# A down-projection by Strassen's seven products in a hybrid encoder layer on one core

## The chip, the cores and the metric

The kernel runs on one core of a Trainium2 chip. The metric is device time in microseconds, the median of several executions. TensorE (PE) multiplies into banks of PSUM; VectorE (DVE) and ScalarE (ACT) read the banks and work on SBUF; GpSimd (POOL) works on SBUF alone; SyncE (SP) issues most DMAs. Each engine carries out its own instructions in order and waits for the others by semaphores.

## The reference, cut to what matters

The layer has a token-mixing sublayer (mLSTM and Mamba-2 branches) and a gated MLP. The change touches the MLP:

```python
u = causal_dwconv(x @ w_up[l], f_conv_w[l], f_conv_b[l])      # width 3 over the tokens
u_gate, u_val = jnp.split(u, 2, -1)
x = layer_norm(ALPHA * x + (jax.nn.silu(u_gate) * u_val) @ w_down[l], ln2_g[l], ln2_b[l])
```

There are 512 tokens, 1024 model columns and D_FF = 2752 hidden features, that is 21.5 tiles of 128. `w_up` is 1024 x 5504 and `w_down` 2752 x 1024, all in float32.

## The kernel before

**Precision.** Each float32 operand is split in two: H, a copy rounded to the type that TensorE takes (a cast on ScalarE), and L, the remainder (a subtraction on VectorE). A product of two operands is three matmuls: H by H, L by H, H by L.

**Weights.** The host lays all weights out as units of 128x1024 in the order of use. `advance` (L132) loads unit after unit into three `raw` buffers (DMA issued by SP, L136), casts it to `wH` (L159) and subtracts to `wL` (L165); `wH` and `wL` have three buffers each. A unit's split waits until TensorE has finished with the unit three before it.

**Up-projection** (the loop over j = 0..20 that calls `feature_major` and `conv_taps`). A gate unit and a value unit of 128 columns each take 24 matmuls (8 tiles of the model dimension, three each) into one bank. Four banks (`mm_bank`) rotate. `conv_taps` (L503) reads a bank three times: ScalarE scales the bank into a `tmp` tile (L505), VectorE adds two shifted taps (L507). ScalarE's SiLU (L1050), VectorE's product (L1051) and a split (L1053, L1054) give the tiles `fH`, `fL` of 128 features by 512 tokens. A last unit `um` holds the half tile of both kinds. `tmp` tiles have eight buffers.

**Down-projection** (`wide_product`, L929, with `tail=5`). All eight banks hold the output: four token tiles c by two column halves hf. Feature tile after feature tile, each bank gets three matmuls of 128x512 (L944); the half tile, stacked as H over L, gets two. The last five feature tiles are done bank by bank, so that the layer norm of a token tile (`wd`, L1087, and the block below it) runs beside the matmuls of the next. The tiles `x1r` hold the residual, read back from DRAM at the end of the up-projection and scaled there (L1076 to L1078).

**Order.** The tile framework's scheduler orders each engine's instructions by a simulated timeline. Inside `in_order(...)` blocks the engines that are named keep the order in which the code is written; the last one covers PE, DVE, ACT and POOL from the last five feature tiles to the end. A pool's buffer is given out again once its last readers are done.

## Time and profile before

| | |
|---|---|
| median of 3 runs | 942.72 us (942.71 to 942.82) |
| profiled execution, its time | 942.7 us |
| its span | 941.0 us |
| TensorE busy | 924.0 us, 98% |
| VectorE, ScalarE, GpSimd busy | 555.0, 382.3, 66.0 us |
| granted TensorE clock, mean | 0.994 |
| DMA | 105.13 MB, 112 GB/s |

The span runs from the first to the last instruction. Rows of a timeline read: start, duration, engine, line, operation, output<-inputs, count, and in brackets the idle time before it and what ended that. Rows of a group end with busy time, mean ns of one, and idle time before. Rows of a stretch (A:B) give its length and for PE, weight load, DVE, ACT and POOL the busy time and count, then the granted clock, the mean busy share of the DMA engines and GB/s. Rows of DMA issues end with the microseconds from issue to landing. In a row of waits stand the total, the count and the longest.

### The profile page before, as it was taken

What the parts mean: (1) busy time and instruction counts of PE and PEld (TensorE: products, weight loads), DVE (VectorE), ACT (ScalarE), POOL (GpSimd) and SP (SyncE); (2) the same over time, 40 slices, a digit from 0 to 9 for tenths busy, and PEclk for the clock granted to TensorE, in tenths of its full rate; (3) what the DMA queues carried; (4) which work ended last, traced back from release to release, by engine and by line L of the source; (5) the groups of instructions that cost most, each with busy time, mean ns of one, the idle gap of its engine ahead of it and who ended that gap; (6) DMA issues with size and microseconds to landing.
All of it is one profiled execution on the core that took longest, in us unless ns stands there. A gap on an engine that the chain in (4) does not pass through costs nothing.

```text
span 941.0 us, 11703 instructions
## 1 busy us (share of the span) xinstructions
PE 924.0 (98%) x4565; PEld 762.3 (81%) x4565; DVE 555.0 (59%) x916; ACT 382.3 (41%) x572; POOL 66.0 (7%) x81
## 2 busy tenths in 40 slices
PE   7999999999999999999999999999999999999996
PEld 4988888888877888888888888888888888878884
DVE  6685889873556465324339467666666556642246
ACT  4456456442664552234122235544444444332121
POOL 3000000211012510000000000000000000000005
PEclk8999999999999999999999999999999999999998
DMA  5334326453232432223334352222322322632212
GB/s 186 105 101 138 109 88 142 123 147 118 90 111 70 139 109 77 102 90 96 106 112 157 112 178 91 90 90 92 109 90 93 110 90 91 251 128 90 95 62 90
DMA packets 46311, 105.13 MB, mean 112 GB/s; under 512 B 4064, under 2 KB 21144, under 8 KB 46256
## 3 DMA queue, kind: packets, MB, share of 16 engines
q1 hardware_dynamic: 45456, 103.30, 34.0%
q0 software_dynamic: 512, 1.07, 0.4%
q8 instruction: 36, 0.59, 0.3%
q14 instruction: 19, 0.16, 0.1%
q10 hardware_dynamic: 288, 0.02, 0.0%
HBM read 100.08 MB, written 4.30 MB: 111 GB/s over the span
## 4 chain that ended last, share of the span: by engine, by line
PE 94%; DVE 2%; DMA 1%; issue 1%; POOL 0%; ACT 0%; DVEq 0%; ACTq 0%; POOLq 0%
PE u L185 23%; PE wd L944 10%; PE g L185 9%; PE z L185 5%; PE o L185 5%; PE v L575 5%; PE xs L185 5%; PE pb L185 5%; PE pa L185 5%; PE wo L944 4%; PE bc L185 4%; PE q L185 2%; PE k L185 2%; PE bc L335 1%; PE up L185 1%
## 5 line engine op out<-in xcount | busy, mean ns | idle before, releaser
L165 DVE TENSOR_TENSOR wL<-raw,wH 128x1024 fp32r<-128x1024 f32 x151 | 186.4, 1238 | 231.3 <-ACT wH L159 229.2
L159 ACT CAST wH<-raw 128x1024 fp32r<-128x1024 f32 x152 | 159.1, 1051 | 285.5 <-PE g L185 62.8
L185 PE MATMUL u<-x1H,wL 128*128 128x512 f32 x312 | 121.4, 389 | 0.0
L185 PE MATMUL u<-x1L,wH 128*128 128x512 f32 x312 | 121.4, 389 | 0.0
L185 PE MATMUL u<-x1H,wH 128*128 128x512 f32 x312 | 121.4, 389 | 0.0
L185 PEld LDWEIGHTS u<-x1H,wH 128*128 128x128 f32 x312 | 58.6, 188 | 12.1
L185 PEld LDWEIGHTS u<-x1H,wL 128*128 128x128 f32 x312 | 58.6, 188 | 12.0
L185 PEld LDWEIGHTS u<-x1L,wH 128*128 128x128 f32 x312 | 58.6, 188 | 11.8
L944 PE MATMUL wd<-wH,fH 128*128 128x512 f32 x168 | 65.5, 390 | 0.8 <-ACT wH L159 0.8
L944 PE MATMUL wd<-wH,fL 128*128 128x512 f32 x168 | 65.4, 389 | 0.0
L944 PE MATMUL wd<-wL,fH 128*128 128x512 f32 x168 | 63.9, 389 | 0.0
L185 PE MATMUL g<-xnH,wH 128*128 128x512 f32 x128 | 50.1, 392 | 0.0
L185 PE MATMUL g<-xnH,wL 128*128 128x512 f32 x128 | 49.8, 389 | 0.0
L185 PE MATMUL g<-xnL,wH 128*128 128x512 f32 x128 | 49.8, 389 | 0.0
L232 POOL TENSOR_TENSOR rs<-ve,mhalf 128x1 f32<-128x1 f32 x12 | 7.6, 629 | 555.8 <-DVE ve L256 555.5
L944 PEld LDWEIGHTS wd<-wH,fH 128*128 128x128 f32 x168 | 31.5, 188 | 7.7 <-ACT wH L159 1.2
L944 PEld LDWEIGHTS wd<-wH,fL 128*128 128x128 f32 x168 | 31.5, 188 | 6.6
L944 PEld LDWEIGHTS wd<-wL,fH 128*128 128x128 f32 x168 | 31.5, 188 | 6.5
L1053 ACT CAST fH<-cg 128x512 fp32r<-128x512 f32 x21 | 13.0, 620 | 53.0 <-DVE cg L1051 53.0
L507 DVE SCALAR_TENSOR_TENSOR cv<-u,par,cv 128x511 f32<-128x511 f32 (+1 forms) x40 | 29.8, 746 | 0.7
L1050 ACT ACTIVATE cg<-cg 128x512 f32<-128x512 f32 x21 | 13.3, 632 | 40.8 <-DVE cg L507 40.8
L507 DVE SCALAR_TENSOR_TENSOR cg<-u,par,cg 128x511 f32<-128x511 f32 (+1 forms) x38 | 28.4, 746 | 0.6
(326 smaller groups left out, 1972.2 us busy)
## 6 DMA issues: line engine op xcount, KB each, us to landing
raw<-in_wts_dram SPq DMA_DIRECT2D x154, 512.0 KB, 3.3
csb<-scr SPq DMA_DIRECT2D x8, 512.0 KB, 7.3
gt<-in_prow_dram SPq DMA_DIRECT2D x12, 256.0 KB, 4.7
xt<-in_x_dram SPq DMA_DIRECT2D x4, 512.0 KB, 6.5
rb<-scr SPq DMA_DIRECT2D x4, 512.0 KB, 5.5
res<-in_x_dram SPq DMA_DIRECT2D x4, 512.0 KB, 5.3
x1d<-res SPq DMA_DIRECT2D x4, 512.0 KB, 2.6
x1r<-x1d SPq DMA_DIRECT2D x8, 256.0 KB, 5.7
```

The lines of the kernel that those rows point to most:

```text
L159: nc.scalar.copy(H, raw)
L165: eng.tensor_tensor(L, raw, H.bitcast(F32), ALU.subtract)
L185: nc.tensor.matmul(ps[:, t0:t1], w_[:, k, :], a_[k][:, t0:t1], start=i == 0, stop=i == 3 * KD - 1)
L232: nc.gpsimd.tensor_tensor(dst, var, epsl[:, :n], ALU.pow)
L335: nc.tensor.matmul(fb[u][:, t], w_[:, k, :], a_[k][:, t], start=n == 1, stop=n == 3 * KD)
L507: nc.vector.scalar_tensor_tensor(dst[:, d:], ps[:, 0:T - d], prm(ws[n - 1 - d], j)[rows], dst[:, d:], ALU.mult, ALU.add)
L575: nc.tensor.matmul(banks[c], a_[k][:, cs_], w_[:, kk, :], start=first and s == 0, stop=last and s == 2)
L944: nc.tensor.matmul(banks[c, hf], a_[:, cs_], w_, start=k == 0 and s == 0, stop=k == n - 1 and s == len(prs) - 1)
L1050: nc.scalar.activation(tg, tg, AF.Silu)
L1053: nc.scalar.copy(H, tg)
```

## The change

Twenty of the feature tiles are multiplied by Strassen's scheme in Winograd's form. With the tokens in halves (256 each), the features in halves (ten tiles each) and the output columns in halves (512 each), the activations are A11, A12, A21, A22 and the weights B11, B12, B21, B22. The sums are S1 = A21 - A22, S2 = S1 - A11, S3 = A11 - A21, S4 = S2 + A12, T1 = B11 + B12, T2 = T1 + B22, T3 = B22 + B12, T4 = T2 + B21; the products P1 = A11 B11, P2 = A12 B21, P3 = S4 B22, P4 = A22 T4, P5 = S1 T1, P6 = S2 T2, P7 = S3 T3. A product covers two token tiles (two banks) and has five steps of two feature tiles, 12 matmuls each. P6 and P7 are accumulated on the bank of P1, P3 on that of P5; after a product the banks are read and added to, or subtracted from, `x1r`. The remaining one and a half feature tiles ("r") are multiplied as before, four matmul groups on four bank pairs.

The four activation sums are made by GpSimd in the up-projection, whose order of units alternates between the feature halves (`UP_ORDER`). They are split (H and L) in the down-projection. The four weight sums are made by DMAs issued by GpSimd from DRAM to DRAM, copies and accumulating ones, in six stages for each of five blocks, two feature tiles to a block; GpSimd keeps the order of the code there. The residual is scaled and shifted in the up-projection and stored to DRAM (`residual`). The whole down-projection stands in an `in_order` block. P4's last three steps run first for token tile 2, then for token tile 3. For token tiles 0 and 1 the last bias is added by an accumulating DMA.

TensorE where the up-projection ends and the down-projection begins, before (`um` is the last up unit, `wd00` the bank of token tile 0 and column half 0, `x1H7` and `x1L7` the activations; the rows ahead are alike in both):

```order
L185 MATMUL um_6491<-x1L7_4420,wH131_6418 128x512
L185 MATMUL um_6491<-x1H7_4412,wL131_6419 128x512
L944 MATMUL wd00_6583<-wH132_6449,fH0_5004 128x512
L944 MATMUL wd00_6583<-wH132_6449,fL0_5005 128x512
L944 MATMUL wd00_6583<-wL132_6450,fH0_5004 128x512
L944 MATMUL wd01_6584<-wH132_6449,fH0_5004 128x512
L944 MATMUL wd01_6584<-wH132_6449,fL0_5005 128x512
```

and now, with what the rows wait for (`dnH20` is the split weight block of P2's step 0, `a2H0` activations of A12, `wdy0` and `wdy1` the two banks of P2):

```order
L178 MATMUL um_6575<-x1H7_4412,wL131_6509 128x512
L1219 MATMUL wdy0_6643<-dnH20_6665,a2L0_5066 128x512
L1219 MATMUL wdy0_6643<-dnL20_6666,a2H0_5065 128x512 [waits DVE_49]
L1219 MATMUL wdy1_6644<-dnH20_6665,a2H0_5065 128x512 [waits DVE_49,Activation_49]
L1219 MATMUL wdy1_6644<-dnH20_6665,a2L0_5066 128x512
```

The first bank pair is now the one that rotates in after `um`: `wdy1` is given `um`'s bank and waits for VectorE and ScalarE at the stage's fourth matmul.

ScalarE near the end, before (`wH152` and `wH153` are the last weight splits, `x1r00` the output tile of token tile 0 and column half 0):

```order
L159 CAST wH150_7073<-raw150_7011 128x1024
L159 CAST wH152_7111<-raw152_7071 128x1024
L159 CAST wH153_7115<-raw153_7101 128x1024
L1115 ACTIVATE x1r00_6541<-x1r00_6541,nb2_0_7160,rs2_6582 128x512
L1115 ACTIVATE x1r01_6545<-x1r01_6545,nb2_0_7160,rs2_6582 128x512
```

and now (`dnH42` to `dnH44` are the splits of P4's steps 2 to 4):

```order
L1053 CAST dnH41_7314<-dn41_7294 128x1024
L1053 CAST dnH42_7334<-dn42_7312 128x1024
L1249 ACTIVATE x1r00_6611<-x1r00_6611,nb2_0_7352,rs2_6636 128x512
L1249 ACTIVATE x1r01_6613<-x1r01_6613,nb2_0_7352,rs2_6636 128x512
L1053 CAST dnH43_7364<-dn43_7332 128x1024
L1053 CAST dnH44_7382<-dn44_7362 128x1024
L1249 ACTIVATE x1r10_6615<-x1r10_6615,nb2_1_7386,rs2_6636 128x512
```

The normalisations of token tile 0 moved ahead of the last two weight splits.

GpSimd in the up-projection had nothing to do before. A turn of it now, with waits (`sum2` holds S1 to S4, `tsum0` to `tsum3` are T1, T2, T3 and T4; a DMA at L1085 accumulates, one at L1087 copies):

```order
L1085 DMA tsum1_5015<-in_wts_dram 128x2x512 [waits DMASW6_49]
L1087 DMA tsum0_5014<-in_wts_dram 128x2x512
L1087 DMA tsum2_5016<-in_wts_dram 128x2x512
L1087 DMA tsum3_5017<-tsum1_5015 128x1024 [waits DMASW7_49]
L1085 DMA tsum0_5014<-in_wts_dram 128x2x512 [waits DMASW0_49]
L1085 DMA tsum2_5016<-in_wts_dram 128x2x512 [waits DMASW4_49,DMASW1_49]
L1103 TENSOR_TENSOR sum2_5006<-cg4_5624,cg14_5701 128x256 [waits DVE_49]
L1104 TENSOR_TENSOR sum2_5006<-sum2_5006,cg4_5624 128x256 [waits Pool_49]
L1105 TENSOR_TENSOR sum2_5006<-cg4_5624 128x256
L1106 TENSOR_TENSOR sum2_5006<-sum2_5006,cg14_5701 128x256 [waits Pool_49]
L1085 DMA tsum3_5017<-in_wts_dram 128x2x512 [waits DMASW5_49,DMASW2_49]
```

The additions that release the `tmp` tiles `cg` stand in one order with DMAs that wait for earlier DMAs (the semaphores DMASW).

The diff, cut to its core:

```diff
+UP_ORDER = [j for i in range(10) for j in (i, i + 10)] + [20]
...
+    def block(k0, hf, i):
+        return wts[DN[k0 + 2 * i]:DN[k0 + 2 * i] + 2, :, 512 * hf:512 * hf + 512].rearrange("u p c -> p u c")
+
+    def weight_sum(stage, i):
...
+        t1, t2, t3, t4 = (t[:, i] for t in tsum)
+        moves = [[(t1, block(0, 0, i), False), (t3, block(10, 1, i), False)],
+                 [(t1, block(0, 1, i), True), (t3, block(0, 1, i), True)],
+                 [(t2, t1, False)], [(t2, block(10, 1, i), True)], [(t4, t2, False)], [(t4, block(10, 0, i), True)]]
+        for dst, src, add in moves[stage]:
+            if add:
+                nc.gpsimd.dma_start(dst, src, accum_op=ALU.add)
+            else:
+                nc.gpsimd.dma_start(dst, src)
+
+    with in_order(ET.Pool):
+        for i, j in enumerate(UP_ORDER):
+            tg = gated(i, j)
+            if i in (3, 5, 7, 9):
+                residual((i - 3) // 2)
...
+                nc.gpsimd.tensor_tensor(s1, low[:, TH:], tg[:, TH:], ALU.subtract)
+                nc.gpsimd.tensor_tensor(s2, s1, low[:, 0:TH], ALU.subtract)
+                nc.gpsimd.tensor_tensor(s3, low[:, 0:TH], low[:, TH:], ALU.subtract)
+                nc.gpsimd.tensor_tensor(s4, s2, tg[:, 0:TH], ALU.add)
...
+            for stage in range(5, -1, -1):
+                if (i - 1 - stage) % 3 == 0:
+                    weight_sum(stage, (i - 1 - stage) // 3)
...
-    wd_tail = wide_product(UX["DN"], fH, fL, 5, "wd", last_stack=True)
+    bX, bY = ([mm_bank(f"wd{n}{i}") for i in range(2)] for n in "xy")
+    bZ, bW = ([sm_bank(f"wd{n}{i}") for i in range(2)] for n in "zw")
+    BANK = {1: bX, 2: bY, 3: bZ, 4: bW, 5: bZ, 6: bX, 7: bX}
+    steps = ([(2, 0), (2, 1), (2, 2), ("r", 0), ("r", 1), (2, 3), (2, 4)] + [(1, i) for i in range(5)]
+             + [(5, i) for i in range(5)]
+             + [(6, 0), (6, 1), (3, 0), (6, 2), (3, 1), (6, 3), (3, 2), (6, 4), (3, 3), (3, 4)]
+             + [(7, i) for i in range(5)] + [(4, i) for i in range(5)])
...
+    def ahead(n):
+        for what, f, m in (("load", load_step, n + 3), ("hl", split_step, n + 2), ("s", sum_step, n + 2)):
...
+        for q in range(2):
+            for m in ms:
+                for s_, (a_, w_) in enumerate(((aH, H), (aL, H), (aH, L))):
+                    nc.tensor.matmul(BANK[p][m], a_[:, q, m * P:(m + 1) * P], w_[:, q, :],
...
+            elif (p, i) == (7, 4):
+                scaled(bX, 2, 0)
+            elif (p, i) == (4, 0):
+                plus(bX, 2, 1, op=ALU.subtract)
+                apply2(0)
+            elif (p, i) == (4, 1):
+                for c in (2, 3):
+                    nc.vector.bn_stats(bn2[c][:, 1, :], x1r[c][1])
+                ahead(len(steps) - 1)
+                apply2(1)
...
+        def last(c):
+            for p, i in steps[-3:]:
+                product(p, i, (c - 2,))
```

## The prediction, made before the changed kernel was run

> **What bounds the kernel now.** I read the page's totals and its chain of waits first, then the busy times of three stretches, then single rows.

> ```profile
> span 941.0 us, 11703 instructions
> PE 924.0 (98%) x4565; PEld 762.3 (81%) x4565; DVE 555.0 (59%) x916; ACT 382.3 (41%) x572; POOL 66.0 (7%) x81
> PE 94%; DVE 2%; DMA 1%; issue 1%; POOL 0%; ACT 0%; DVEq 0%; ACTq 0%; POOLq 0%
> PE wd L944 <- ACT wH L159: 0.8, 1, 0.8
> 600.00:700.00 100.00, 100.00 (x442) 82.80 (x441) 63.54 (x79) 45.65 (x59) 0.95 (x1) 1.00 0.29 95
> 812.00:830.00 18.00, 17.22 (x77) 13.95 (x75) 14.31 (x23) 5.01 (x8) 0.00 (x0) 1.00 0.69 264
> 830.00:900.00 70.00, 70.00 (x309) 57.95 (x310) 19.42 (x17) 15.48 (x16) 0.00 (x0) 1.00 0.33 107
> ```

> TensorE is the bound: 94% of the chain, and inside the up-projection (600 to 700) and the down-projection (830 to 900) it is never idle. There VectorE is busy 63.5% and 28%, ScalarE 46% and 22%, the DMA engines 29% and 33%. Only its work, its waits and the tail behind its last matmul count. The time of this execution is 942.7 us against a span of 941.0, so 1.7 lies around the span; the median of the runs is 942.72.

> A matmul must not be priced at its row's 389 ns, because rows overlap. The price is the distance between starts:

> ```profile
> 807.25 0.39 PE L185 MATMUL um<-x1H,wH 128*128 128x512 f32 x1
> 812.69 0.39 PE L944 MATMUL wd<-wH,fH 128*128 128x512 f32 x1
> 931.42 0.39 PE L944 MATMUL wd<-wL,fHm 128*128 128x512 f32 x1
> L944 PE MATMUL wd<-wH,fH 128*128 128x512 f32 x168 | 65.5, 390 | 0.8 <-ACT wH L159 0.8
> L944 PE MATMUL wd<-wH,fL 128*128 128x512 f32 x168 | 65.4, 389 | 0.0
> L944 PE MATMUL wd<-wL,fH 128*128 128x512 f32 x168 | 63.9, 389 | 0.0
> L944 PE MATMUL wd<-wH,fHm 128*128 128x512 f32 x8 | 3.1, 389 | 0.0
> L944 PE MATMUL wd<-wL,fHm 128*128 128x512 f32 x8 | 3.1, 389 | 0.0
> ```

> The 24 matmuls of the last up unit (`um`) go from 807.25 to 812.69: 5.44 / 24 = 0.2267 us each. The down-projection has 3 x 168 + 2 x 8 = 520. Its slots run from 812.69 to 931.42 + 0.23 = 931.65, which is 118.96 us; 520 x 0.2267 = 117.88, so 1.1 us are stalls.

> **The change, term by term.** *Matmuls.* Twenty of the 21.5 feature tiles go through seven products of 5 steps with 12 matmuls (420) in place of 20 x 24 = 480; the rest keeps 24 + 16 = 40. So 460 x 0.2267 = 104.27 us instead of 118.96: 14.7 less, the 1.1 of stalls included. By the rows' 389 ns the sixty would be worth 23.3, which is the mistake to avoid.

> *The seam at the end of the up-projection.* In the kernel before, the bank of `um` was the seventh that the down-projection wrote, 18 matmuls on. Now the first step writes `wdy0` and `wdy1`, and `wdy1` is the bank of `um`: its first matmul is the fourth of the stage and waits until `um` is read. The reading stands on ScalarE and VectorE behind the split of weight block (2,2), whose buffer `um`'s own weights held. One unit earlier in the trace the same sequence reads:

> ```profile
> 725.42 0.39 PE L185 MATMUL u<-x1H,wL 128*128 128x512 f32 x1
> 725.62 1.05 ACT L159 CAST wH<-raw 128x1024 fp32r<-128x1024 f32 x1 [0.30 <-PE u L185]
> 726.58 0.78 ACT L505 ACTIVATE cg<-u,par 128x512 f32<-128x512 f32 x1
> 726.71 1.23 DVE L165 TENSOR_TENSOR wL<-raw,wH 128x1024 fp32r<-128x1024 f32 x1 [0.66 <-ACT wH L159]
> 727.85 1.53 DVE L507 SCALAR_TENSOR_TENSOR cg<-u,par,cg 128x511 f32<-128x511 f32 x2
> ```

> The unit's last matmul starts at 725.42, its slot ends at 725.65, the second tap ends at 729.38: 3.73 us after the slot. The new stage has 3 matmuls (0.68) to do meanwhile; with 0.05 for the semaphore TensorE stands 3.1 us. Nothing hides it.

> *Steps of half the length.* A step lasts 12 x 0.2267 = 2.72 us and needs one weight block (512 KB) split, in twenty steps a sum of activations as well:

> ```profile
> L165 DVE TENSOR_TENSOR wL<-raw,wH 128x1024 fp32r<-128x1024 f32 x18 | 21.9, 1224 | 49.0 <-ACT wH L159 49.0
> L159 ACT CAST wH<-raw 128x1024 fp32r<-128x1024 f32 x19 | 19.8, 1052 | 52.0 <-PE wd L944 46.8 <-DMA raw<-in_wts_dram 5.0 <-PE um L185 0.3
> L150 DVE TENSOR_TENSOR wL<-raw,wH 128x512 fp32r<-128x512 f32 x2 | 1.4, 688 | 4.0 <-ACT wH L149 4.0
> L149 ACT CAST wH<-raw 128x512 fp32r<-128x512 f32 x2 | 1.2, 617 | 4.6 <-DMA raw<-in_wts_dram 4.6
> raw<-in_wts_dram SPq DMA_DIRECT2D x154, 512.0 KB, 3.3
> csb<-scr SPq DMA_DIRECT2D x8, 512.0 KB, 7.3
> x1r<-x1d SPq DMA_DIRECT2D x8, 256.0 KB, 5.7
> rsb<-rsd POOLq DMA_DIRECT2D x4, 256.0 KB, 4.2
> ```

> VectorE: 1.22 + 0.69 = 1.91 of 2.72; ScalarE 1.05 + 0.62 = 1.67. Bank readings (two of 0.7) come at nine ends of products and push a split back by at most 1.4 + 0.7 us, while a split stands 2.5 us before its matmul: no stall. The loads need 524 KB per 2.72 us, 193 GB/s; the stretch from 812 to 830 moved 264 with engines 69% busy. With four raw buffers a block is asked for about 10.4 us before its matmul and split in 2.3, so landing may take 8 us against the 3.3 of this load. I take no cost; bounds 0 and, at the 7.3 of `csb`, 0.

> *Weight sums and activation sums in the up-projection.* GpSimd gets 40 additions of 128x256 and 40 DMAs of 512 KB, 20 of them accumulating, in one order.

> ```profile
> 261.55 1.44 POOL L729 TENSOR_TENSOR qs<-qT,sib 128x256 f32<-128x256 f32 x2
> 325.25 3.03 POOL L862 DMA_DIRECT2D rsb<-rsd  x4 [2.33 <-DMA rsd<-rs_y]
> ```

> An addition costs 0.72, an issue 0.75. An iteration is two units, 10.88 us; three of them (32.6) hold 8 DMAs and, through the waits on their own forerunners, a chain of one copy and two accumulations. No row shows an accumulation: at least the 4.2 of `rsb`, at most three such passes (two reads, one write), 12.6, beside a copy at the 7.3 of `csb`. That chain is 12.6 to 32.5, under 32.6 even at the top, so GpSimd keeps pace and TensorE doesn't wait: 0.

> The additions slow VectorE (rows of the tail below), by up to 0.8 times their 29 us; with `residual`'s eight passes of 1.22 its share rises from 63% to about 75% and stays under TensorE. The sixteen passes over `x1r` at the seam (L1077, L1078) go; they were hidden.

> *Last product.* Let F be the end of product 7. ScalarE now has the two normalisations of token tile 0 (0.76 each) ahead of the split of block (4,3), and they wait on VectorE: scaling 1.5, split (4,2) 1.2, two subtractions 1.4, shift 0.2, so they run F + 4.5 to 6.0; then H of (4,3) to 7.05, L to 8.2, two statistics, L of (4,4) to 10.8. Product 4 goes token tile by token tile, so (4,3) is due at F + 2 x 2.72 + 6 x 0.2267 = 6.8: 0.3 late for H, 0.8 more for L; (4,4) another 1.2. Stall 2.3 us.

> *Tail.* Before, from the last matmul's start:

> ```profile
> 931.84 0.69 DVE L1090 SCALAR_TENSOR_TENSOR x1r<-x1r,wd 128x512 f32<-128x512 f32 x1 [0.56 <-PE wd L944]
> 932.57 0.69 DVE L1091 BATCH_NORM_STATS2 bn<-x1r 128x6 f32<-128x512 f32 x1
> 933.29 0.21 DVE L254 BATCH_NORM_AGGREGATE mv<-bn 128x2 f32<-128x12 f32 x1
> 933.54 0.15 DVE L256 TENSOR_SCALAR ve<-mv 128x1 f32<-128x1 f32 x1
> 933.77 0.55 POOL L232 TENSOR_TENSOR rs<-ve,mhalf 128x1 f32<-128x1 f32 x1
> 934.43 1.14 DVE L1122 SCALAR_TENSOR_TENSOR x1r<-x1r,mv,gt 128x512 f32<-128x512 f32 x2
> 935.48 2.08 DVE L1124 SCALAR_TENSOR_TENSOR x1r<-x1r,rs,gt 128x512 f32<-128x512 f32 x2
> 936.23 1.05 POOL L1119 TENSOR_TENSOR x1r<-x1r,gt 128x256 f32<-128x256 f32 x1
> ```

> VectorE ends 6.14 us after that start (937.56) and the span 3.44 later. The same 768 columns take 1.14 alone and 2.08 beside GpSimd. Now token tile 2 keeps VectorE until 1.9 after the last start (its chain of additions, statistics, power, ScalarE and product runs from F + 13.3 to 17.6, the last matmul starts at F + 15.7); then 0.72 + 0.72 + 0.25 + 0.2 + 0.65 + 4 x 0.68 = 5.3: 7.2, or 7.8 where GpSimd's last addition lies beside it. I take 7.5: 1.4 more.

> *Sum.* 941.0 - 14.7 + 3.1 + 2.3 + 1.4 = 933.1 span, 934.8 us; 0.8% faster.

> **Rivals.** *GpSimd falls behind* (slower). Place: its order in the up-projection. It decides from 2 x accumulation + copy = 32.6 us on. At 18 and 8 a turn takes 44 and the debt over the four to five turns is about 50; the eight `tmp` buffers carry 27 of it, then convolutions, splits and TensorE wait: 934.8 + 23 = 958. For it: GpSimd is the one queue whose chain has no spare beyond the upper bound, and no accumulation was ever seen. Against: 18 is four times the 4.2 of `rsb`. 9%.

> *Loads land late in the down-projection.* From 8 us on each further microsecond delays every round of the four buffers, and 37 loads make about nine rounds, the first of them covered: 8 us for one, so at 9 it is 934.8 + 7 = 942, no gain. For it: 193 GB/s instead of 107 and rows of 2 KB; against: 264 moved at the seam, and there 5.7. 11%.

> *The clock drops at the seam.*

> ```profile
> 11.60 0.47 PE L273 MATMUL xnt<-ident,xt 128*128 128x128 f32 x1 [3.76 <-DVE xt L297]
> 10.00:15.00 5.00, 1.99 (x8) 1.70 (x9) 3.80 (x10) 1.80 (x2) 2.17 (x3) 0.62 0.83 338
> 15.00:20.00 5.00, 5.00 (x25) 3.53 (x24) 4.30 (x7) 4.12 (x11) 2.37 (x1) 0.69 0.00 0
> ```

> After 3.76 idle us the granted clock was 0.62 and 0.69 for 10 us: 5 x 0.38 + 5 x 0.31 = 3.5 us. A gap of 3.1 may do the same: 938.3. Against: that gap was longer and thin work followed. 9%. [...]

> *The waits are shorter* because ScalarE or VectorE reach the reading of `um` or the split of (4,3) earlier than my order has it: without both, 934.8 - 5.4 = 929.4; with half, 932. 11%.

> **How the numbers follow.** Forecast 60%, its own range 932.5 to 937.5; the four rivals 9, 11, 9 and 11%. Range 930.5 to 942: it holds the forecast, the dropped clock, most of the short waits and the mild end of late loads; outside lie GpSimd's debt and loads over 9 us. About 0.2% (1.9 us) is what a measurement can tell from no change. Faster: forecast, clock, short waits and a third of the late loads less a little, 81%; within 0.2% 4%; slower 15% (GpSimd's 9 and half of the late loads).

> **What would show it.** Right: 460 matmuls 0.2267 apart in the down-projection; a wait of TensorE on VectorE of about 3.1 us at its fourth matmul, clock 1.00 after it; two or three waits on ScalarE and VectorE (sum 2.3) in the last three steps; VectorE done 7 to 8 us after the last matmul starts; an up-projection of unchanged length. Wrong: idle TensorE between 600 and 807, accumulations landing after 12 us, weight loads over 8 us, or matmuls further apart than 0.2267.

## The result, and the profile after

The changed kernel takes 931.96 us (median of four runs, 930.04 to 933.64) against 942.72 (942.66 to 942.82): a ratio of 0.9885, 95% interval 0.9866 to 0.9904. The forecast was 934.8, its own range 932.5 to 937.5, the whole range 930.5 to 942. The time lies where the rival of the shorter waits stood. The runs of the new kernel lie 3.6 us apart, those of the old one 0.16; that was not foreseen.

The page of the changed kernel (its profiled execution took 933.64 us): span, busy totals, chain, and two rows of the costliest groups and of the DMA issues.

```profile
span 931.6 us, 11841 instructions
PE 911.9 (98%) x4505; PEld 750.8 (81%) x4505; DVE 592.0 (64%) x953; ACT 404.0 (43%) x605; POOL 139.7 (15%) x159
PE 91%; DMA 3%; issue 2%; DVE 2%; ACT 1%; POOL 1%; SPq 0%; DVEq 0%; ACTq 0%; POOLq 0%
...
L1085 POOL DMA_DIRECT2D tsum<-in_wts_dram x20 | 23.2, 1209 | 35.9 <-DMA tsum<-tsum 27.3
...
tsum<-in_wts_dram POOLq DMA_DIRECT2D x30, 512.0 KB, 8.1
dn<-tsum SPq DMA_DIRECT2D x20, 512.0 KB, 3.9
dn<-in_wts_dram SPq DMA_DIRECT2D x15, 512.0 KB, 4.1
tsum<-tsum POOLq DMA_DIRECT2D x10, 512.0 KB, 5.5
```

TensorE still is the bound, but the chain now has 3% of DMA and 1% of ScalarE in it. Who TensorE waited for from the up-projection on (total, times, longest), and one row of VectorE's waits:

```profile
PE u L178 <- DVE wL L158: 1.2, 2, 0.7
PE u L178 <- ACT wH L156: 1.1, 1, 1.1
PE wdw L1219 <- DVE dnL L1054: 0.7, 1, 0.7
DVE x1a L1065 <- DMA x1a<-x1d: 15.2, 4, 7.4
```

There is no wait of 3.1 us at the seam; there are three in the up-projection (`u`), where none was expected; and 0.7 in the last product instead of 2.3. The timeline gives the corners:

```profile
583.18 0.36 PE L178 MATMUL up<-x1H,wH 128*128 128x256 f32 x1
815.73 0.39 PE L1219 MATMUL wdy<-dnH,a2H 128*128 128x512 f32 x1
920.97 0.39 PE L1219 MATMUL wdw<-dnL,a2H 128*128 128x512 f32 x1
927.16 1.40 DVE L1316 SCALAR_TENSOR_TENSOR x1r<-x1r,rs,gt 128x512 f32<-128x512 f32 x2
```

Against the corners of before (583.42, 812.69, 931.42, VectorE's end at 937.56, span 941.0) this makes:

| stretch | before | after | change | predicted |
|---|---|---|---|---|
| up to the up-projection | 583.42 | 583.18 | -0.24 | 0 |
| up-projection, to the first matmul of the down-projection | 229.27 | 232.55 | +3.28 | 0 |
| first to last matmul start of the down-projection | 118.73 | 105.24 | -13.49 | -9.3 |
| last matmul start to VectorE's end | 6.14 | 7.59 | +1.45 | +1.4 |
| VectorE's end to the span's end | 3.44 | 3.04 | -0.40 | 0 |
| sum | 941.0 | 931.6 | -9.40 | -7.9 |

Two misses with opposite signs, +3.3 us in the up-projection and -4.2 in the down-projection (-13.49 against -9.3), stand behind a total that looks good. This execution is the longest of the four; the median lies 1.7 us lower.

### The profile page after: what moved, and what is told of

The parts are those of the page before. It is cut to its first block, busy times and chain, and to the rows that moved or that the text cites. A ratio compares the mean times of both kernels' runs of the same rounds, so it can differ in the third digit from the quotient of the medians.

```text
span 931.6 us, 11841 instructions
## 1 busy us (share of the span) xinstructions
PE 911.9 (98%) x4505; PEld 750.8 (81%) x4505; DVE 592.0 (64%) x953; ACT 404.0 (43%) x605; POOL 139.7 (15%) x159
## 4 chain that ended last, share of the span: by engine, by line
PE 91%; DMA 3%; issue 2%; DVE 2%; ACT 1%; POOL 1%; SPq 0%; DVEq 0%; ACTq 0%; POOLq 0%
PE u L178 20%; PE g L178 9%; PE z L178 5%; PE o L178 5%; PE v L568 5%; PE xs L178 5%; PE pb L178 5%; PE pa L178 5%; PE wdx L1219 4%; PE wo L937 4%; PE bc L178 4%; PE wdz L1219 3%; PE q L178 2%; PE k L178 2%; DMA x1a<-x1d 2%
## 5 line engine op out<-in xcount | busy, mean ns | idle before, releaser
L158 DVE TENSOR_TENSOR wL<-raw,wH 128x1024 fp32r<-128x1024 f32 x131 | 164.5, 1259 | 158.9 <-ACT wH L156 156.8
L156 ACT CAST wH<-raw 128x1024 fp32r<-128x1024 f32 x131 | 137.0, 1048 | 224.2 <-PE g L178 62.8
L1054 DVE TENSOR_TENSOR dnL<-dn,dnH 128x1024 fp32r<-128x1024 f32 x35 | 43.3, 1237 | 26.9 <-ACT dnH L1053 22.7
L225 POOL TENSOR_TENSOR rs<-ve,mhalf 128x1 f32<-128x1 f32 x12 | 9.5, 795 | 321.3 <-DVE ve L249 321.3
L1053 ACT CAST dnH<-dn 128x1024 fp32r<-128x1024 f32 x35 | 36.8, 1054 | 43.7 <-PE wdx L1219 19.8
L1048 ACT ACTIVATE cg<-cg 128x512 f32<-128x512 f32 x21 | 13.3, 633 | 56.4 <-DVE cg L500 56.4
L1085 POOL DMA_DIRECT2D tsum<-in_wts_dram x20 | 23.2, 1209 | 35.9 <-DMA tsum<-tsum 27.3
L178 PEld LDWEIGHTS g<-xnL,wH 128*128 128x128 f32 x128 | 24.1, 188 | 4.9
L178 PEld LDWEIGHTS g<-xnH,wL 128*128 128x128 f32 x128 | 24.0, 188 | 4.9
L178 PEld LDWEIGHTS g<-xnH,wH 128*128 128x128 f32 x128 | 24.0, 188 | 4.9
L178 PE MATMUL z<-xnH,wH 128*128 128x512 f32 x64 | 25.8, 403 | 0.0
## 6 DMA issues: line engine op xcount, KB each, us to landing
raw<-in_wts_dram SPq DMA_DIRECT2D x132, 512.0 KB, 3.4
tsum<-in_wts_dram POOLq DMA_DIRECT2D x30, 512.0 KB, 8.1
dn<-tsum SPq DMA_DIRECT2D x20, 512.0 KB, 3.9
dn<-in_wts_dram SPq DMA_DIRECT2D x15, 512.0 KB, 4.1
tsum<-tsum POOLq DMA_DIRECT2D x10, 512.0 KB, 5.5
csb<-scr SPq DMA_DIRECT2D x8, 512.0 KB, 7.0
xt<-in_x_dram SPq DMA_DIRECT2D x4, 512.0 KB, 6.4
rb<-scr SPq DMA_DIRECT2D x4, 512.0 KB, 5.8
```

The source lines that it names most:

```text
L156: nc.scalar.copy(H, raw)
L158: eng.tensor_tensor(L, raw, H.bitcast(F32), ALU.subtract)
L178: nc.tensor.matmul(ps[:, t0:t1], w_[:, k, :], a_[k][:, t0:t1], start=i == 0, stop=i == 3 * KD - 1)
L225: nc.gpsimd.tensor_tensor(dst, var, epsl[:, :n], ALU.pow)
L1048: nc.scalar.activation(tg, tg, AF.Silu)
L1053: nc.scalar.copy(H, t)
```

## Experiments

Each kernel was timed beside the kernel before on the same chip. The first four share a chip, so do the next four, and the last three; the kernel before took 942.71, 942.65 and 942.14 us there, so distances across these groups are good to about half a microsecond.

**Where do the 3.3 us of the up-projection come from?** VectorE around the first gap of TensorE in the changed kernel, with the load's issue by SyncE and the late matmul:

```profile
617.40 0.69 DVE L1049 TENSOR_TENSOR cg<-cg,cv 128x512 f32<-128x512 f32 x1
618.56 0.42 DVE L1054 TENSOR_TENSOR a11L<-cg,a11H 128x256 fp32r<-128x256 f32 x1 [0.47 <-ACT a11H L1053]
619.18 0.33 SPq L1064 DMA_DIRECT2D x1a<-x1d  x1
626.39 1.22 DVE L1065 TENSOR_TENSOR x1a<-x1a,ln1g 128x1024 f32<-128x1024 f32 x1 [7.40 <-DMA x1a<-x1d]
627.53 1.22 DVE L158 TENSOR_TENSOR wL<-raw,wH 128x1024 fp32r<-128x1024 f32 x1
628.81 0.50 PE L178 MATMUL u<-x1H,wL 128*128 128x512 f32 x1 [0.70 <-DVE wL L158]
```

VectorE stands 7.4 us in front of the residual's multiplication, whose load was issued at 619.18; the split that TensorE needs (627.53) is queued behind it. The four passes stand at 608.7, 626.4, 638.8 and 653.4 us, that is in iterations 1 to 4 of the loop. The code calls `residual` in iterations 3, 5, 7 and 9: outside an `in_order` block the scheduler had moved them forward, each right behind its own load. Since the four share a buffer, each load stands behind the store before it: SyncE issues it 2.9 to 6.4 us after that store. Three kernels went together; the changed one once more as the yardstick.

> The changed kernel once more, beside the others of this group, to see how far its own runs scatter. All theories: 930 to 933.7 us, as its first four runs.

Measured 931.41 us (930.69 to 931.97). VectorE's wait on `x1a` is 12.7 us in it, TensorE's gaps are shorter (0.9 us of waits in all), the up-projection is 231.07 long.

`late_residual`:

```diff
     def residual(c):
         t = ff.tile([P, 1024], F32, tag="raw", name=f"x1a{c}", bufs=1)
+        made = nc.cur_bb.bb.instructions[-1]
         nc.sync.dma_start(t, x1d[:, c, :])
         nc.vector.tensor_tensor(t, t, g1, ALU.mult)
+        tc.add_manual_dep(nc.cur_bb.bb.instructions[-1], made.name,
+                          mybir.DependencyInfo(mybir.DependencyClass.NoSync, mybir.DependencyReason.DATA), reason="late")
```

> Only edit: the first pass of VectorE over x1a may not stand earlier in VectorE's order than where the code has it, behind the product of iteration 3, 5, 7 and 9 (in the changed kernel the scheduler had put the passes into iterations 1 to 4, each right behind its load). Theory A, the residual's loads: VectorE stood 15.2 us on x1a, TensorE lost 2.9 us through that. Now no wait of VectorE on x1a, no gap of TensorE between 600 and 815, up-projection 229.3 to 229.7 us long instead of 232.6, time 928.5 to 929.5, and the runs agree within 0.6 us. Rival B, the weight sums: their transfers and the additions on GpSimd hold VectorE and the weight loads up, wherever the residual stands; gaps of 2 to 3 us stay, time 931 to 933 with the same scatter.

Measured 930.29 us, 930.11 to 930.46. The stretches of the page, changed kernel first, then this one (length and PE, weight load, DVE, ACT and POOL busy, clock, DMA share, GB/s):

```profile
620.00:640.00 20.00, 19.30 (x85) 15.64 (x84) 11.39 (x13) 6.39 (x9) 4.73 (x5) 1.00 0.71 209
640.00:660.00 20.00, 18.33 (x80) 14.54 (x79) 13.93 (x18) 4.91 (x7) 2.56 (x3) 1.00 0.78 252
```

```profile
620.00:640.00 20.00, 20.00 (x90) 16.58 (x89) 14.46 (x16) 8.25 (x12) 6.88 (x6) 1.00 0.72 216
640.00:660.00 20.00, 20.00 (x90) 16.58 (x89) 15.90 (x17) 7.71 (x11) 11.26 (x10) 1.00 0.77 233
```

No row of VectorE waits for `x1a` any more, TensorE is busy throughout although the DMA share is the same, and the up-projection lasts 229.27 us (583.17 to 812.44), what it lasted before the change. The runs lie 0.35 us apart, those of the changed kernel beside it 1.3. Theory A holds in place and kind. The gain in the time is smaller than expected, 1.1 us: the expectation took the loss of one execution, the longest of the four.

`no_accum`:

```diff
-            if add:
-                nc.gpsimd.dma_start(dst, src, accum_op=ALU.add)
-            else:
+            if not add:
                 nc.gpsimd.dma_start(dst, src)
```

> The 20 accumulating DMAs of the weight sums are left out (the 20 copies stay), so products 4 to 7 multiply wrong weights; the residual stays as in the changed kernel. Theory A: the loads of x1a land in 4 to 6 us instead of 7.5, VectorE's wait on them falls from 15.2 to 5 to 9 us but is still there, TensorE loses 0 to 1.5 us; time 929 to 931. Rival B: the wait of VectorE on x1a nearly gone, no gap of TensorE between 600 and 815, time 928.5 to 929, no scatter.

Measured 931.56 us (931.13 to 933.17), above both expected ranges and level with the changed kernel. A gap of TensorE is still there, 1.05 us at 640, behind waits of VectorE on `x1a` of 10.1 us in three, though the longest of them is now 5.3 us instead of 7.4:

```profile
PE u L178 <- DVE wL L158: 1.1, 1, 1.1
DVE x1a L1065 <- DMA x1a<-x1d: 10.1, 3, 5.3
```

With the accumulations gone the loss and the scatter stay; with the residual held back and all accumulations there, both go. Rival B falls.

**Was there a wait at the seam to be had?** `seam_banks`:

```diff
-    bX, bY = ([mm_bank(f"wd{n}{i}") for i in range(2)] for n in "xy")
+    bX = [mm_bank(f"wdx{i}") for i in range(2)]
+    bY = [mm_bank("wdy0"), pg]        # pg is um's bank
```

> Only edit: the second bank of product 2 is the bank of um (the prediction had it so, the trace shows that it was another). Theory A, the prediction's step with the bank put right: TensorE waits 3.0 to 3.2 us on VectorE at the fourth matmul of the down-projection, granted clock 1.00 behind it; time 3.1 over the changed kernel's. Rival, the clock drops after the gap: 6 to 7 over. Rival, the reading of um is reached earlier once TensorE waits for it: 1 to 2 over.

Measured 937.35 us (935.15 to 938.89), 5.9 over the changed kernel beside it. The wait of TensorE, and the stretches around it:

```profile
PE um L1220 <- DVE cgm L500: 3.0, 1, 3.0
813.24:816.65 3.41, 1.07 (x5) 0.56 (x3) 2.78 (x4) 1.72 (x2) 0.00 (x0) 1.00 0.95 328
816.65:823.47 6.82, 6.13 (x15) 4.86 (x16) 3.14 (x4) 2.91 (x4) 0.00 (x0) 0.50 0.87 301
823.00:830.00 7.00, 7.00 (x31) 5.76 (x30) 2.78 (x3) 2.11 (x2) 0.95 (x1) 0.97 0.48 158
```

The wait is the predicted one, 3.0 us. But the granted clock is 0.50 from 816.65, inside the wait, to 823.47: the 15 matmuls from 817.34 to 823.71 take 6.4 us instead of 15 x 0.2267 = 3.4. So here the wait of 3.0 us costs 5.9, about twice its length, and the rival of the dropped clock is what this kernel shows, just under the 6 to 7 us that it gave. Two of its six runs are only 3.8 over; they may have kept the clock, but neither their times nor their mean clocks (0.992, among 0.989 to 0.994 of the others) can show it.

`seam_short` shortens the same gap by three matmuls; beside the edits of `seam_banks` and `late_residual` it has:

```diff
-        for q in range(2):
-            for m in ms:
+        for q, m in [(q, m) for m in ms for q in range(2)] if (p, i) == (2, 0) else [(q, m) for q in range(2) for m in ms]:
+            if True:
```

> As seam_banks (the second bank of product 2 is um's) with the residual held back, and the first step of product 2 takes both feature tiles of its first bank before the second bank, so that um's bank is due at the seventh matmul: the gap is 0.68 us shorter, 2.35. Theory, the clock falls where a window of some length with little work ends inside the gap, so a shorter gap does it seldom or never: time 2.4 over late_residual's 930.3, granted clock 1.00 after the gap. Rival, any gap over 2 us does it: 5 us over.

Measured 932.94 us (932.79 to 933.01), 2.65 over `late_residual`; wait and clock:

```profile
PE um L1223 <- DVE cgm L500: 2.4, 1, 2.4
812.01:815.43 3.42, 1.88 (x9) 1.22 (x7) 2.66 (x4) 1.81 (x3) 0.00 (x0) 1.00 0.99 337
815.43:818.84 3.41, 2.60 (x11) 2.17 (x12) 1.43 (x3) 2.41 (x4) 0.00 (x0) 1.00 0.99 360
```

**What sets the end?** The three kernels of this part hold the residual back as `late_residual` does. `late_tail` changes how token tile 2 is finished while token tile 3 is multiplied:

```diff
-        norm2(2)
-        nc.vector.tensor_tensor(x1r[2][0], x1r[2][0], gt2[0][0], ALU.mult)
...
+        t, q = x1r[2]
+        nc.vector.scalar_tensor_tensor(t, t, mv2[:, 2, 0:1], gt2[0][0], ALU.subtract, ALU.mult)
+        nc.scalar.activation(q, q, AF.Identity, bias=shift(2), scale=rs2[:, 2:3])
+        nc.vector.scalar_tensor_tensor(t, t, rs2[:, 2:3], gt2[1][0], ALU.mult, ALU.add)
...
         finish2(3)
-        nc.vector.tensor_tensor(x1r[2][0], x1r[2][0], gt2[1][0], ALU.add)
```

> The residual held back as in late_residual, and the last token tiles finished in another order: the first half of token tile 2 is scaled by VectorE alone (mean and gamma as soon as the mean is there, while GpSimd makes the power; then the power and beta), so that ScalarE is out of its way and no VectorE pass of token tile 2 stands behind the last matmul. Theory (VectorE's passes behind the last matmul set the end: 7.6 us in the changed kernel, of which 1.4 are token tile 2's and about 1.0 are lost beside GpSimd's): VectorE ends 5.2 to 6.2 us after the last matmul starts, time 928.2 to 929.2 against late_residual's 930.3. Rival, the stores at the end set it, not VectorE: 930 to 930.4.

Measured 929.02 us (928.3 to 929.6). Rows of VectorE from the end of token tile 2's statistics on, and GpSimd's last addition:

```profile
916.93 0.74 DVE L1307 SCALAR_TENSOR_TENSOR x1r<-x1r,mv,gt 128x512 f32<-128x512 f32 x1
918.13 0.16 DVE L1246 SCALAR_TENSOR_TENSOR nb<-mv,rs 128x1 f32<-128x1 f32 x1 [0.46 <-POOL rs L225]
918.21 0.75 DVE L1309 SCALAR_TENSOR_TENSOR x1r<-x1r,rs,gt 128x512 f32<-128x512 f32 x1
918.87 0.68 DVE L1234 TENSOR_TENSOR x1r<-x1r,wdw 128x512 f32<-128x512 f32 x1
...
920.63 1.41 DVE L1317 SCALAR_TENSOR_TENSOR x1r<-x1r,mv,gt 128x512 f32<-128x512 f32 x2
921.75 1.40 POOL L1313 TENSOR_TENSOR x1r<-x1r,gt 128x512 f32<-128x512 f32 x1
921.95 2.41 DVE L1320 SCALAR_TENSOR_TENSOR x1r<-x1r,rs,gt 128x512 f32<-128x512 f32 x2
```

The last matmul starts at 917.85, VectorE ends at 924.36, 6.5 us later instead of 7.6 (5.2 to 6.2 were expected), and is nearly never idle. The time is in the range expected. The last two passes take 2.41 beside GpSimd's last addition (921.75 to 923.15), the two before it 1.41 alone.

`late_tail_split`:

```diff
+                ahead(len(steps) - 1)
                 for c in (2, 3):
                     nc.vector.bn_stats(bn2[c][:, 1, :], x1r[c][1])
-                ahead(len(steps) - 1)
```

> late_tail, and the split of block (4,4) ahead of the two statistics of token tiles 2 and 3. Theory (the 0.7 us that TensorE waits for the L of (4,4), and the two slots of 0.34 around it, come from these statistics on VectorE): the wait goes, matmul end 0.9 us earlier, but the statistics and what stands behind them come 0.3 later, so VectorE is then the bound of the tail; 0.2 to 0.8 under late_tail. Rival, VectorE is the bound already: no change or up to 0.4 over.

Measured 929.22 us (928.61 to 929.33): no gain. The wait of TensorE is gone and the last matmul starts 104.30 us after the first of the stage instead of 105.25, but VectorE's last pass ends 111.76 us after that first matmul in both kernels. The rival holds: with the better order VectorE is the bound of the tail, and 0.95 us of TensorE's stalls cost nothing.

`late_plain` does the last three steps of product 4 for both token tiles together:

```diff
-        last(2)
+        for p, i in steps[-3:]:
+            product(p, i)
         finish2(2)
-        last(3)
```

> The residual held back as in late_residual, product 4 undivided: its last three steps for both token tiles together. Theory (the order by token tile hides the additions, statistics and scaling of token tile 2 behind the 18 matmuls, 8.2 us, of token tile 3): VectorE ends 9 to 10 us after the last matmul starts instead of 7.6, time 1.5 to 2.5 over late_residual's 930.3. Rival, VectorE is as long occupied either way because ScalarE and GpSimd cover token tile 2: within 0.5.

Measured 931.35 us (930.85 to 931.7), 1.1 over `late_residual`. VectorE ends 10.0 us after the last matmul starts, as the theory has it; but TensorE is done 1.2 us earlier (916.48), for the wait of 0.7 in the last steps and the longer slots around it are gone. The order by token tile is worth 1.1 us (across two groups, so give or take half a microsecond), under the 1.5 to 2.5 expected.

**How far is GpSimd from falling behind?** `twice_accum`:

```diff
-                nc.gpsimd.dma_start(dst, src, accum_op=ALU.add)
+                for _ in range(2):
+                    nc.gpsimd.dma_start(dst, src, accum_op=ALU.add)
```

> The residual held back, and each of the 20 accumulating DMAs of the weight sums issued twice, the second behind the first (the weight sums are then wrong). It tells how far the changed kernel is from the point where GpSimd's order holds the up-projection up. By the prediction's rival: a chain of four accumulations and a copy, 4 x 8.7 + 6.9 = 41.7 us by the landings of late_residual, exceeds the 32.6 of three iterations by 9.1, in four to five turns about 41, of which the eight buffers carry 27: about 14 us over late_residual's 930.3, with TensorE idle late in the up-projection; more if the landings grow. Against it: the copies and accumulations of two blocks overlap, the chain counts less than that: 0 to 3 over. A third way: the DMA engines, 0.93 busy already, delay the weight loads: TensorE waits on ScalarE's split and that on raw.

Measured 1001.59 us (998.33 to 1003.59), 71 over `late_residual` where about 14 were expected. Waits of GpSimd in the up-projection of `late_residual` first, then the rows of `twice_accum`:

```profile
POOL sum L1106 <- DVE cg L1049: 53.0, 8, 12.0
POOL tsum L1088 <- DMA tsum<-tsum: 33.3, 6, 9.0
POOL tsum L1090 <- DMA tsum<-in_wts_dram: 18.4, 4, 8.5
POOL tsum L1088 <- DMA tsum<-in_wts_dram: 8.5, 6, 2.9
```

```profile
POOL tsum L1089 <- DMA tsum<-in_wts_dram: 144.3, 25, 9.4
ACT cg L498 <- POOL sum L1109: 43.4, 3, 17.3
PE u L178 <- ACT wH L156: 19.5, 3, 10.8
PE wdy L1223 <- ACT dnH L1053: 24.8, 2, 15.1
```

The chain is the rival's: GpSimd waits for its own DMAs, its additions come late, ScalarE has no free `tmp` buffer for the next unit, TensorE waits for ScalarE's split. In `late_residual` the additions wait 53.0 us for VectorE's products: that is GpSimd's spare. Twice the accumulations bring 184 us of waits on its own DMAs (144.3, and 22.9 and 16.7 in two more rows) instead of 60, so 124 more, of which 53 are covered; 71 are left, the measured difference. (The issues of the twenty added DMAs and a clock that fell to 0.69 to 0.96 after the longer gaps are in it too, so the match is partly luck.) The expected 14 took the turn of three iterations for 41.7 us. In the chain of this trace one copy of each turn (`tsum<-tsum`) starts at 637.55, 694.42, 751.19, 802.94 and 852.07, so a turn takes 49 to 57 us against the 32.6 allowed: from one to the next six transfers stand one behind another and not five, with GpSimd's issues and additions between them. The third way falls: the weight loads of the up-projection land in 3.5 us as in `late_residual`.

**Is the better version better?** `after_beside` is the changed kernel, `late_tail_again` is `late_tail`.

> The changed kernel beside the next one on the same chip: 930 to 933.7 us.

> late_tail once more, beside the changed kernel: 928.3 to 929.6 us, that is 2.0 to 3.0 under it, if residual and tail are what they seemed; within 1.0 of it, if the earlier distance lay in the chip.

Measured 932.18 us (930.29 to 933.06), ratio to before 0.9896 (0.988 to 0.9913), and 929.20 (928.69 to 929.42), 0.9861 (0.9846 to 0.9875). The intervals do not meet; 3.0 us, as expected. The version with the residual held back and the reordered tail beats both kernels. Of the changed kernel's twelve runs none is under 930.04, of this version's eight none over 929.6.

## Why the prediction was right, and where it was not

*Matmuls: right.* The 460 matmuls stand 0.2267 us apart: 815.73, 815.96, 816.19, 816.41. In `late_tail_split` first and last start are 104.30 apart, 459 x 0.2267 = 104.06. The row's mean of 389 ns would have promised 8.6 us more.

*The seam: wrong.* The step that failed is "`wdy1` is the bank of `um`" (the section on the change says the same). A wait on VectorE and ScalarE stands at that matmul in the program, and I took it for the wait on `um`'s readers by counting banks in rotation. The banks are not handed out so: in the built program `um` has the fourth bank and the first product has the two that had been free longest; `um`'s bank went to `wdx1`, which is first written 39 matmuls into the stage. The trace says the same without the program: the fourth matmul starts at 816.41, the reading of `um` goes on until 819.46:

```profile
816.41 0.39 PE L1219 MATMUL wdy<-dnH,a2H 128*128 128x512 f32 x1
816.67 0.77 ACT L498 ACTIVATE cgm<-um,par 128x512 f32<-128x512 f32 x1
817.93 1.53 DVE L500 SCALAR_TENSOR_TENSOR cgm<-um,par,cgm 128x511 f32<-128x511 f32 x2
```

The price of the wait itself was right (3.0 in `seam_banks` against 3.1), though the rows it was read from lie 87 us ahead of the seam and not one unit. Its consequence was not: I had the clock staying whole as the likelier case, by my own estimate, because the gap of 3.76 us in the trace of before was longer and thin work followed it. In `seam_banks` a gap of 3.19 us from slot end (814.15) to start (817.34) did halve the clock, and one of 2.51 (813.73 to 816.24 in `seam_short`) did not. The 3.41 us that ended in the fall held 1.07 us of matmuls (the row of `seam_banks` from 813.24). In `twice_accum` the clock falls six times, behind stretches of 3.41 us with 0 to 0.87 us of matmuls, and does not fall behind those with 1.77 us and more; where in between it turns these traces do not show.

*Steps of half the length: right.* No wait of TensorE between 824 and 912; VectorE is busy 23.20 of 30 us from 870 to 900, ScalarE 17.31; loads land in 3.9 and 4.1 us against 8 allowed.

*Weight and activation sums: right, and incomplete.* Accumulations and first copies land in 8.1 us, copies between sums in 5.5; two and one make 21.7, inside the 12.6 to 32.5 bounded. The issue of an accumulating DMA takes 1.2 us on GpSimd, not 0.75. GpSimd kept pace, with 53 us to spare in `late_residual`; `twice_accum` shows how near that rival lay, for a doubling of the accumulations loses 71 us. What the step missed stands in the same paragraph, in the words "with `residual`'s eight passes of 1.22 its share rises". I counted those passes as busy time alone. Each of them also waits for a load, in VectorE's order, in front of the splits of TensorE's next unit; the code's place in the loop was taken for the place in VectorE's order. This is the whole of the +3.28, for with the residual held back the up-projection has the 229.27 of before. Over three profiled executions of the changed kernel, VectorE's wait on `x1a` of 15.2, 12.7 and 11.7 us goes with an up-projection of 232.55, 231.07 and 230.06 and with times of 933.64, 931.97 and 930.29 (in the last the work ahead was also 0.9 shorter). That it is most of the scatter too is likely but not shown: on one chip four runs of the changed kernel lie 2.8 us apart and four of `late_tail_again` 0.7, but those of `late_tail`, which also holds the residual back, lie 1.3 apart.

*Last product: over-sized.* One wait of 0.7 and longer slots around it, 1.2 in all, where 2.3 stood; VectorE and ScalarE reach the split of (4,3) and (4,4) about 1 us earlier than reckoned. And the terms of TensorE's stall and of the tail were added as if both counted. `late_tail_split` shows that in the better tail they do not add: VectorE's chain runs through both.

*Tail: right.* 7.59 us against 7.5 from the last matmul's start to VectorE's end; the stores behind it took 0.4 less than before.

The number came out near because a stall of 3 us that I predicted was not there and one of 1 to 3 us that I did not predict was. That the median lies below the forecast's own range, where the rival of the shorter waits had it, is luck: the wait at the seam was not shorter by that rival's reason, it did not exist, and part of its length was lost elsewhere.

## What to carry to other kernels

A pass that waits for a DMA is not priced by its duration: here VectorE stood up to 7.4 us in front of a pass of 1.22, until the load had landed, with the split for TensorE behind both. Where a scheduler chooses the place, look at the place it chose, not at the line in the code. Which wait stands behind a semaphore is read from the buffer's address or from the trace, not by counting a rotation. At the end of a kernel add up the engine that finishes last; stalls of the other engine before it may cost nothing, as the 0.95 us of TensorE's did in `late_tail`.

## What was not expected of the hardware

A gap of TensorE of 3.0 us halved the granted clock for 6.8 us and so cost 5.9 in the median, while a gap of 2.4 cost 2.7 with the clock whole: 0.7 us of gap, and another place of it among the stretches of 3.41 us, went with 3.3 us of time. That GpSimd's additions slow VectorE's passes was expected; they are slowed themselves as well: one of 128x256 takes 0.73 us alone and up to 1.72 beside VectorE, a split of 1.22 became 1.72 beside them. And the DMA engines carried weight loads, sums and copies at a busy share of 0.92 from 660 to 700 us (256 GB/s) without a weight load late:

```profile
803.96 0.73 POOL L1103 TENSOR_TENSOR sum<-cg,cg 128x256 f32<-128x256 f32 x1 [11.53 <-DVE cg L1049]
805.91 1.72 DVE L1054 TENSOR_TENSOR dnL<-dn,dnH 128x1024 fp32r<-128x1024 f32 x1 [0.66 <-ACT dnH L1053]
806.51 1.72 POOL L1106 TENSOR_TENSOR sum<-sum,cg 128x256 f32<-128x256 f32 x1
660.00:700.00 40.00, 40.00 (x178) 33.13 (x177) 27.95 (x35) 19.55 (x27) 20.16 (x22) 1.00 0.92 256
```
